# One decoder layer on one core, its program put in order by the scheduler's second timing model

## The chip, the cores and the metric

The kernel runs on one core of one Trainium2 chip. The metric is the device time of one execution in microseconds (us): 3150.36 us before the change, the median of three runs. In what follows PE is TensorE (the matmul engine), DVE is VectorE, ACT is ScalarE, POOL is GpSimd and SP is SyncE, which issues most of the transfers.

## The reference: what is computed

One layer for 2048 tokens of width 1024, all in float32. One projection feeds four mixers; their outputs pass through an output matrix and a layer norm; then come a mixture of 32 experts and a gated embedding, and a second layer norm.

```
u   = x @ W_in  (one combined projection; columns split among four parallel head groups)
y_A = RWKV-7 time mixing (4 heads x 64)       y_B = chunked gated linear attention (4 heads, dk 32, dv 64)
y_C = chunkwise mLSTM (4 heads x 64)          y_D = multi-head latent attention with decoupled rotary key (4 heads, dv 64)
x   = LN(alpha * x + concat(y_A, y_B, y_C, y_D) @ W_out)
x   = LN(alpha * x + HMoE(x) + sigmoid(x W_g + b_g) * (p[i] @ W_p))
HMoE: top-1 expert group, then top-2 SwiGLU experts inside that group.
```

## The kernel before

**Products.** A float32 product is made in three passes over rounded halves (`mm3`, L57 to L61: high by high at L59, and the two mixed ones at L60 and L61). The halves are made by `split`: a cast on ACT (L51) and a subtraction on DVE or POOL (L52).

**Order of the work.** The program is written with Tile: the code issues instructions in an order, and a scheduler then makes each engine's list. It is a list scheduler. It keeps a model of when each engine comes free and when each result is there; when an engine is free by that model, it takes, of the instructions that are ready by it, the one with the best priority, and an earlier place in the code is a better priority. So the code's order ranks the work, and the model's durations and delays decide how much lower-ranked work is put between two steps of a chain. On the chip every engine then works through its list in order and waits at each instruction for what that needs. Memory is taken from pools that are opened and closed in the code; tiles of a pool that is opened over the room of a closed one wait until the old tiles are done with.

**Mixers.** `layer()` steps through the projections in two halves of the tokens, in blocks of up to 256 columns (`proj`, L102), whose products go to the PSUM tile pbank. Between blocks it takes steps of the RWKV mixer from a generator (`rwkv`, L620), which uses the PSUM tiles abank and bbank. `rwkv_pre` (L380) prepares a piece of 256 tokens: sums of squares at L415, a chain of small DVE operations for their inverse roots (rk_iv, L68 to L73, called from there) and the decay factors, and products with the result at L423. `rwkv_b` (L526) solves a tile's triangular systems in dependent sub-steps (L541, L545, L550, L555, L562, L568). At block `LAST_AT` of the second half the rest of RWKV is written, its pools are closed, and the attention's normalized inputs and latents (`mla_norms` L1094 with the column sums at L1106, `mla_latents` L1118; PSUM tile sbank) are written between the last blocks:

```
            if n == L.LAST_AT:
                for _ in r:
                    pass
                rw.close()
                L.mla_pools(mla)
...
                L.mla_early(early)
                d = L.mla()
            if 0 <= n - L.LAST_AT < 4:
                next(d)
                L.gla_pre(n - L.LAST_AT)
        pr.close()
        L.gm_pools(gm)
        early.close()
        L.mla_more(mla)
```

After `pr.close()` the mLSTM mixer (`mlstm`, L924; PSUM tile cbank, state update L970 to L975) and the gated linear attention (`gla`, L733; PSUM tile gbank, first product L745, masked copy L747) get their pools in the room of the projections. `L.mla_more` opens the attention's pool in the room of the latents' pool, so no query of the attention starts before the last latents are made. Then 16 rounds of eight steps of attention (queries `mla_query` L1182 with scores at L1205, keys and values `mla_attend` L1225), one step of GLA and one of mLSTM follow.

**Output and experts.** `out_proj` (L1384, product at L1408) and `ple` (L1557) follow, and then `moe` (L1851). In a step of its loop, expert e's first block of 128 tokens goes through the gate and up weights (`moe_gu`, L1794, 48 products at L1801); a second block only if it exists, behind a branch at L1922; the down weights of expert e-1 follow (`moe_dn`, L1827, products at L1833, copies of the result on ACT at L1840). The hidden values m_t and the next tokens m_xg are turned by PE at L1350 and split again by L51 and L52. The weights are cast on ACT (L1771) and their low halves made on DVE or POOL (L1772). The branch at L1928 looks for third blocks on four engines. At last `finish` (L2117) and `norm2` (L2143) write the output.

Of the kernel before, what the change touches and what calls it, by code (L numbers as in the profile page):

```python
# [20 lines left out]
D = 1024  # L21
# [9 lines left out]
class Layer:  # L31
# [44 lines left out]
    # feature-major column tiles of w_in (start column, width)  # L76
# [4 lines left out]
    # columns that the token shift mixes, with their place in its weights  # L81
# [20 lines left out]
    def proj(self, h, blocks):  # L102
        """one half of the tokens against some of the columns, a block at a time"""
# [91 lines left out]
    # the columns that a causal convolution and silu follow  # L195
    CONV = "mq0", "mq1", "mk0", "mk1"

    def conv(self, i, p, y, more):
        """the taps carry a factor 1/2"""
# [73 lines left out]
    def sigmoid(self, out, in_, bias=0.0):  # L273
        """out = 0.5 + 0.5 tanh((in + bias2)/2), bias = bias2 / 2"""
        self.nc.scalar.activation(out, in_, AF.Tanh, bias=bias, scale=0.5)
        self.nc.gpsimd.tensor_scalar(out, out, 0.5, 0.5, op0=OP.mult, op1=OP.add)
# [34 lines left out]
    def rwkv_consts(self):  # L311
# [28 lines left out]
        # masks over [j, i]: same chunk of 64, strict / inclusive, block off the 32-diagonal  # L340
# [19 lines left out]
        # row mu of partition quarter s holds row m = 4 mu + s of the transposed inverse  # L360
# [7 lines left out]
        # products of a tile's tokens, zero between its two chunks  # L368
# [11 lines left out]
    def rwkv_pre(self, q):  # L380
        """scaled operands of the chunks and the inverses of the diagonal 32-blocks"""
# [112 lines left out]
    def rwkv_a(self, q, tt):  # L494
        """token-major operands and the masked products of a tile's chunks, four heads together"""
# [30 lines left out]
    def rwkv_b(self, q, tt):  # L526
        """solves, the chain over the chunks, the tile's outputs"""
# [92 lines left out]
    def rwkv(self):  # L620
        """the group in steps: operands run ahead of the products, and these ahead of the chain"""
# [45 lines left out]
    def log_sigmoid(self, z, out, t):  # L667
        """out = min(z, 0) - ln(1 + exp(-|z|)) for z in SBUF"""
# [22 lines left out]
    def gla_pre(self, q):  # L691
        """queries and keys times their chunk's decays, which go out to memory"""
# [86 lines left out]
    def gla_general(self):  # L779
        """Token by token, for decays too strong for the chunks' common scale."""  # L780
# [67 lines left out]
    def mlstm_gates(self):  # L848
        """gates of all chunks of 128, rows 16 h + c, and the running maxima"""
        nc = self.nc  # L850
        with ExitStack() as ctx:
# [39 lines left out]
            # own chunk's decay on the channels of each head  # L891
# [117 lines left out]
    def rope_tables(self):  # L1009
        """cos and sin (negated for the first half of a head's pairs) of position * frequency, for four heads' rows"""  # L1010
# [36 lines left out]
    def mla_consts(self):  # L1047
# [4 lines left out]
        # the heads' first 64 columns; their rotary columns; these with the pairs swapped  # L1052
# [10 lines left out]
        # the heads' key columns, then their value columns  # L1063
# [16 lines left out]
        # adds the two halves of the rows  # L1080
# [13 lines left out]
    def mla_norms(self, q):  # L1094
        """one over the latents' norms"""
# [22 lines left out]
    def mla_latents(self, q, cn, rs):  # L1118
        """latents over their norms; from them the values of all heads, and their queries and keys, which go out to memory"""
# [62 lines left out]
    def mla_query(self, hd, q):  # L1182
        """queries in two parts with the negated row maxima below them, in steps"""
# [11 lines left out]
        # any value near a row's maximum serves its softmax alike: the leading parts give it  # L1195
# [29 lines left out]
    def mla_attend(self, hd, q):  # L1225
        """even key tiles' products in the upper half of the rows, odd ones' in the lower half, at the same time"""
# [48 lines left out]
    def mla(self):  # L1275
        """the attention of a block of queries in steps, the next block's queries and keys made beside it"""
# [24 lines left out]
        for i, (hd, q) in enumerate(blocks):  # L1301
            while at <= i:
                at = next(ahead, 99)
            for _ in self.mla_attend(hd, q):
                work += self.LEAD
                # a head's keys lie over those of the head before the last
# [12 lines left out]
    ALPHA = 2.0 ** 0.25  # L1319

    def late_pools(self, ctx):
        """first norm's outputs in pairs of tiles, over them later an expert's gate and up weights; transposed blocks"""
        self.rc = self.pool(ctx, "rc")
        self.wgu = self.pool(ctx, "m_gu", 8)
        self.hl = self.pool(ctx, "hl", 2)
        self.psb = self.pool(ctx, "ps_b", 2, space=PSUM)
        self.mark = {}
# [4 lines left out]
    def weights(self, parts, n, scale=None, pool=None):  # L1332
        """128 rows of weights, put side by side, in leading and trailing parts"""
# [8 lines left out]
    def transpose_split(self, src, hi, lo, spread=False):  # L1342
        """[128, n] to [128, n/128, 128] in leading and trailing parts, rows 0 .. 63 and 64 .. 127 by turns in case of spread"""
# [113 lines left out]
    def pick(self, vals, mx, io, n, k, name):  # L1457
        """lowest index among the entries equal to the maximum, and its one-hot"""
# [11 lines left out]
    def route(self, t0, n, lg):  # L1470
        """tokens of tiles t0 .. t0 + n from logits [128, n, 36]"""
# [43 lines left out]
    def route_place(self, r):  # L1515
        """slots in the experts' lists, behind those of the earlier tiles"""
# [30 lines left out]
    # columns of router and gate side by side, in groups that fill a bank  # L1547
# [735 lines left out]
```

## Time and profile before

| what | value |
|---|---|
| median of three runs | 3150.36 us (3146.23 to 3152.82) |
| span of the profiled execution, first to last instruction | 3146.7 us |
| mean granted TensorE clock in it | 0.935 of full speed |
| PE busy | 2840.9 us, 90% of the span |
| DVE, ACT, POOL busy | 62%, 39%, 28% |
| DMA | 443.17 MB, mean 141 GB/s |

The profile gives the profiled execution's span and no other time of it; the median of the runs shown lies 3.7 us above that span. The span falls into the projections with RWKV (0 to about 909 us), the rest of the projections with the attention's latents (to 1064 and, with the first steps of mLSTM and GLA, 1103 us), the attention with mLSTM and GLA (to about 1585 us), the output projection and the gates (to about 2037 us), the experts (to about 3010 us), and the end. A busy share averages over these; so the prediction reads each stage by itself: PE's busy time, its granted clock, and what ended its waits.

### The profile page before, as it was taken

Reading aid. Unit: us, or ns where it says so; the run is one execution under the profiler, and the core shown is the slowest. Engines: PE = TensorE matmul, PEld = TensorE weight load, DVE = VectorE, ACT = ScalarE, POOL = GpSimd, SP = SyncE. Lnnn points to the kernel's source line nnn. Section 1 sums busy time; section 2 is a strip of 40 time slices with the busy share of each in tenths; the row PEclk is TensorE's granted clock in tenths of the full one; section 3 lists DMA queues with packets and bytes.
Section 4 is the critical chain, followed back from the end, with each engine's and each line's share of the span. In section 5 each row is a group of like instructions: output and inputs, shape, how many; then the busy total and the mean of one; then the engine's idle time right before and its main releaser. Section 6 shows DMA issues by size and latency. Waiting matters only on the chain. (4 is left out here: it accounts for less than half of the span.)

```text
span 3146.7 us, 42893 instructions
## 1 busy us (share of the span) xinstructions
PE 2840.9 (90%) x15420; PEld 2248.3 (71%) x15421; DVE 1955.0 (62%) x4094; ACT 1225.4 (39%) x2001; POOL 896.7 (28%) x552
## 2 busy tenths in 40 slices
PE   8999999998999899999999998789889988998883
PEld 6888888777877665566577797677667766776662
DVE  6366543566555466766656643467576767666869
ACT  4223232222134332323310121166575756666753
POOL 1000100111010033324421200346355545554525
PEclk9999999999998898989999998899999999999996
DMA  6332143122133612200243412188587867777873
GB/s 189 104 87 75 48 129 92 51 56 59 49 93 132 189 33 69 58 27 17 88 143 132 141 60 60 41 295 275 181 269 233 294 216 237 267 251 225 287 243 134
DMA packets 287054, 443.17 MB, mean 141 GB/s; under 512 B 84088, under 2 KB 152040, under 8 KB 286760
## 3 DMA queue, kind: packets, MB, share of 16 engines
q1 hardware_dynamic: 272200, 397.78, 38.3%
q0 software_dynamic: 14560, 41.47, 5.4%
q8 instruction: 184, 3.01, 0.4%
q14 instruction: 110, 0.90, 0.1%
HBM read 350.52 MB, written 96.50 MB: 142 GB/s over the span
## 5 line engine op out<-in xcount | busy, mean ns | idle before, releaser
L1801 PE MATMUL m_g<-m_g,xhl 128*128 128x512 f32 x2032 | 516.6, 402 | 14.7 <-PEq L1928 8.0
L1801 PEld LDWEIGHTS m_g<-m_g,xhl 128*128 128x128 f32 x2032 | 373.6, 191 | 105.9 <-issue 29.8
L1772 DVE TENSOR_TENSOR m_g<-m_raw,m_g 128x1024 fp32r<-128x1024 f32 x188 | 263.7, 1429 | 124.3 <-ACT m_g L1771 78.9
L1771 ACT CAST m_g<-m_raw 128x1024 fp32r<-128x1024 f32 x252 | 255.3, 1057 | 120.8 <-PEq L1928 105.3
L1833 PE MATMUL m_y<-m_dh,m_h 128*128 128x512 f32 x672 | 236.0, 415 | 24.6 <-PEq L1928 6.1
L59 PE MATMUL pbank<-xh,wh 128*128 128x512 f32 x544 | 220.7, 406 | 11.5 <-DVE us L209 8.2
L60 PE MATMUL pbank<-xl,wh 128*128 128x512 f32 x544 | 219.3, 403 | 0.0
L61 PE MATMUL pbank<-xh,wl 128*128 128x512 f32 x544 | 218.3, 402 | 0.0
L51 ACT CAST xhl<-bank 128x512 fp32r<-128x512 f32 x204 | 118.2, 607 | 251.6 <-PE bank L1350 244.0
L1772 POOL TENSOR_TENSOR m_g<-m_raw,m_g 128x1024 fp32r<-128x1024 f32 x64 | 182.8, 2940 | 89.6 <-ACT m_g L1771 50.5
L1408 PE MATMUL wide<-wt,xhl 128*128 128x512 f32 x768 | 183.4, 397 | 3.6 <-ACT xhl L51 3.6
L1772 POOL TENSOR_TENSOR m_dl<-m_raw,m_dh 128x1024 fp32r<-128x1024 f32 x64 | 177.9, 2814 | 22.1 <-ACT m_dh L1771 21.9
L1833 PEld LDWEIGHTS m_y<-m_dh,m_h 128*128 128x128 f32 x672 | 134.9, 201 | 58.7 <-issue 9.0
L1408 PEld LDWEIGHTS wide<-wt,xhl 128*128 128x128 f32 x768 | 143.7, 189 | 40.1 <-ACT xhl L51 7.4
L1248 POOL TENSOR_TENSOR mla_acc<-mla_acc,mla_pt 128x512 f32<-128x512 f32 (+3 forms) x112 | 135.7, 1212 | 117.4 <-ACT mla_pt L1246 101.1
L52 DVE TENSOR_TENSOR xhl<-bank,xhl 128x512 fp32r<-128x512 f32 x204 | 136.4, 685 | 49.3 <-ACT xhl L51 47.0
L1847 POOL DMA_INDIRECT accd<-m_y,m_put x47 | 94.6, 2013 | 249.6 <-ACT m_y L1840 135.5
L1588 PE MATMUL gate<-wt,xhl 128*128 128x354 f32 (+1 forms) x864 | 152.1, 333 | 14.3 <-DVE wide L1593 7.8
L1246 ACT ACTIVATE mla_pt<-sbank 128x512 f32<-128x512 f32 (+3 forms) x160 | 85.1, 533 | 202.7 <-PE sbank L1242 118.0
L1588 PEld LDWEIGHTS gate<-wt,xhl 128*128 128x128 f32 x864 | 144.1, 193 | 16.5 <-DVE wide L1593 8.6
L1833 PE MATMUL m_y<-m_dl,m_h 128*128 128x512 f32 x376 | 153.9, 409 | 0.0
L59 PE MATMUL pbank<-wh,xh 128*128 128x256 f32 x512 | 151.2, 295 | 0.0
(635 smaller groups left out, 6340.8 us busy)
## 6 DMA issues: line engine op xcount, KB each, us to landing
m_raw<-in_moe_w_down SPq DMA_DIRECT2D x64, 1024.0 KB
m_raw<-in_moe_w_gate SPq DMA_DIRECT2D x126, 512.0 KB
m_raw<-in_moe_w_up SPq DMA_DIRECT2D x126, 512.0 KB
wraw<-in_w_in SPq DMA_DIRECT2D x80, 256.0 KB
o_x<-in_x SPq DMA_DIRECT2D x16, 512.0 KB
x1d<-m_g SPq DMA_DIRECT2D x16, 512.0 KB
accd<-wide SPq DMA_DIRECT2D x16, 512.0 KB
m_raw<-accd SPq DMA_DIRECT2D x7, 1024.0 KB
```

What stands on the lines that cost most here:

```text
L51: nc.scalar.copy(hi, src)
L52: (eng and nc.gpsimd or nc.vector).tensor_sub(lo, src, hi.bitcast(F32))
L59: nc.tensor.matmul(out, lh, rh, start=start, stop=False)
L60: nc.tensor.matmul(out, lh, rl, start=False, stop=False)
L61: nc.tensor.matmul(out, ll, rh, start=False, stop=stop)
L1248: (nc.vector if kt in self.SUMS else nc.gpsimd).tensor_add(acc[:, c0 * 128:512], acc[:, c0 * 128:512], pt[:, 0:n])
L1408: nc.tensor.matmul(p[:, j], a[:, k], W[k][bb][:, j * 512:j * 512 + 512], start=k == 0 and i == 0, stop=k == 7 and i == 2)
L1588: nc.tensor.matmul(p[:, 0:n], a[:, k], b[:, o:o + n], start=k == 0 and i == 0, stop=k == 7 and i == 2)
L1771: self.nc.scalar.copy(h[:, i], raw[:, i])
L1772: lo_eng.tensor_sub(l[:, i], raw[:, i], h[:, i].bitcast(F32))
L1801: self.mark["pe"] = self.nc.tensor.matmul(banks[:, j], a, b[:, k % 2, j * 512:j * 512 + 512], start=k == 0 and i == 0, stop=k == 7 and i = ...
L1833: self.nc.tensor.matmul(p[:, j], a, b[:, k % 2, j * 512:j * 512 + 512], start=k == 0 and i == 0, stop=k == 3 and i == len(ps) - 1)
```

## The change

The context in which the whole program is built is told to use the scheduler's second timing model, which follows the instructions in a more detailed timeline:

```diff
-    with tile.TileContext(nc) as tc:
+    with tile.TileContext(nc, schedule_with_timeline_sim=True) as tc:
```

The rest of the difference drops comments and docstrings. No instruction is written differently and the priorities are the same; each engine's list comes out in another order. PE's list has 12520 lines of difference between the two orders, of some 10700 rows. Three places:

**PE in RWKV's solves.** Here PE's list stands in the second half of the tokens, in `rwkv_b`, from the last product of one sub-step (L550) over the next (L555) to the first of the one after (L562); pbank rows are the projections' products. Before:

```order
L550 MATMUL bbank<-xx,am_1029 128x128
L61 MATMUL pbank<-xh,wl 128x512
L59 MATMUL pbank<-xh,wh 128x512
L60 MATMUL pbank<-xl,wh 128x512
L61 MATMUL pbank<-xh,wl 128x512
L555 MATMUL bbank<-v_6281,dt_1022 128x128 x4
L59 MATMUL pbank<-xh,wh 128x512
L60 MATMUL pbank<-xl,wh 128x512
L61 MATMUL pbank<-xh,wl 128x512
L59 MATMUL pbank<-xh,wh 128x512
L60 MATMUL pbank<-xl,wh 128x512
L562 MATMUL bbank<-am_1028,xx 64x128
```

And now, with the first and the last of the rows that stand between; "..." stands for rows of the same three lines:

```order
L550 MATMUL bbank<-xx,am_1029 128x128
L60 MATMUL pbank<-wl,xh 128x256
L61 MATMUL pbank<-wh,xl 128x256
L59 MATMUL pbank<-wh,xh 128x256
...
L59 MATMUL pbank<-wh,xh 128x256
L555 MATMUL bbank<-v_6281,dt_1022 128x128 x4
L60 MATMUL pbank<-wl,xh 128x256
...
L60 MATMUL pbank<-wl,xh 128x256
L562 MATMUL bbank<-am_1028,xx 64x128
```

Before, four projection products stand in the first gap and five in the second; now there are 33 and 28. Over the 16 solves the mean goes from 3.4 to 18.8 in the first gap and from 5.8 to 23.4 in the second. Between L415 and L423, of which there are eight pairs, it was 24 to 60 and is 38 to 96. RWKV's last product moves from well ahead of the projections' end to that end.

**PE at the end of the projections.** The sbank rows of L1106 are the column sums of `mla_norms`, 48 in all; mla_x holds the attention's inputs, and cbank rows belong to mLSTM. Before, they stand among the projections:

```order
L60 MATMUL pbank<-xl,wh 128x512
L1106 MATMUL sbank<-ones_8179,mla_x 128x1 x4
L61 MATMUL pbank<-xh,wl 128x512
L59 MATMUL pbank<-xh,wh 128x512
L60 MATMUL pbank<-xl,wh 128x512
L1106 MATMUL sbank<-ones_8179,mla_x 128x1 x4
L61 MATMUL pbank<-xh,wl 128x512
L59 MATMUL pbank<-xh,wh 128x512
L60 MATMUL pbank<-xl,wh 128x512
L1106 MATMUL sbank<-ones_8179,mla_x 128x1 x4
```

And now; the first row here is the last projection product of all:

```order
L61 MATMUL pbank<-wh,xl 128x256
...
L950 MATMUL cbank<-ident,c_k 128x128
L950 MATMUL cbank<-ident,c_z 128x128
L1106 MATMUL sbank<-ones_8179,mla_x 128x1 x24
L956 MATMUL cbank<-c_v,c_am 128x65 x4
L959 MATMUL cbank<-ml_st_8075,c_a 128x130
L959 MATMUL cbank<-ml_st_8076,c_q 128x130
L1127 MATMUL sbank<-ident,mla_rs 128x128 x8
L970 MATMUL cbank<-c_v,ml_kw 128x130 x2
L933 LDWEIGHTS identb
```

No row of L1106 is ahead of the projections' last product any more, and the latents (L1147 to L1170) follow these. From that product to the first score of the attention (L1205) PE's list held 26 products into cbank and 22 into gbank before; now it holds 199 of all 304 into cbank, 49 of all 165 into gbank, and 140 into sbank.

**ACT in a step of the expert loop.** m_y is a block's result, m_dh the high half of an expert's down weights, m_h the turned hidden values and xhl the turned tokens. Before:

```order
L1840 COPY m_y<-m_y 128x512
L1771 CAST m_g<-m_raw 128x1024 x2
L51 CAST m_h<-bank 128x4x2x64
L1771 CAST m_dh<-m_raw 128x1024 x2
L1840 COPY m_y<-m_y 128x512
L51 CAST xhl<-bank 128x4x2x64 x2
L1771 CAST m_dh<-m_raw 128x1024
L1902 UNCONDITIONAL_BRANCH
L1771 CAST m_dh<-m_raw 128x1024
L1968 UNCONDITIONAL_BRANCH
```

And now, the same step:

```order
L1840 COPY m_y<-m_y 128x512
L1771 CAST m_dh<-m_raw 128x1024 x4
L1840 COPY m_y<-m_y 128x512
L51 CAST m_h<-bank 128x4x2x64
L51 CAST xhl<-bank 128x4x2x64
L1902 UNCONDITIONAL_BRANCH
L1817 ACTIVATE m_t<-m_g_18055 128x512
L51 CAST xhl<-bank 128x4x2x64
L1968 UNCONDITIONAL_BRANCH
```

Of the four casts into m_dh two stood between the two copies of m_y, behind m_h's split, and two behind xhl's. Now all four stand between the copies and ahead of both splits, and the second half of xhl's split stands behind m_t (L1817), which takes the next expert's first block from PE. On PE, 2 to 10 of the 48 products of L1801 of a first block stood behind the branch on the second block before; now all 48 are ahead of it.

## Rows read from the trace of the kernel before

**Rows 1.** The page: span and busy time of the engines.
```profile
span 3146.7 us, 42893 instructions
...
PE 2840.9 (90%) x15420; PEld 2248.3 (71%) x15421; DVE 1955.0 (62%) x4094; ACT 1225.4 (39%) x2001; POOL 896.7 (28%) x552
```

**Rows 2.** By stage: us; busy of PE, PEld, DVE, ACT, POOL; clock, DMA share, GB/s.
```profile
0.00:909.00 909.00, 855.62 (x5991) 721.43 (x5993) 503.62 (x1494) 246.17 (x509) 79.58 (x101) 0.96 0.30 84
909.00:1064.00 155.00, 147.45 (x731) 114.50 (x730) 85.53 (x221) 66.83 (x111) 5.71 (x9) 0.89 0.43 134
1064.00:1103.00 39.00, 30.72 (x133) 20.82 (x131) 17.06 (x51) 11.84 (x27) 0.18 (x2) 0.69 0.82 245
1103.00:1607.00 504.00, 479.45 (x2292) 302.29 (x2291) 325.81 (x746) 156.80 (x319) 188.40 (x152) 0.92 0.19 55
```

**Rows 3.** Waits of PE, 0 to 909 us: total us, times, longest.
```profile
PE abank L423 <- DVE rk_iv L73: 16.8, 5, 5.0
...
PE abank L423 <- DVE eend L457: 4.6, 1, 4.6
PE abank L423 <- DVE gi L484: 4.4, 1, 4.4
```

**Rows 4.** PE in order of time, 700 to 716 us: start, us, instruction, idle before.
```profile
715.65 0.69 PE L423 MATMUL abank<-ident,rk_iv 128*64 128x128 f32 x4 [4.65 <-DVE eend L457]
```

**Rows 5.** Busy time by stretch around that gap; columns as in rows 2.
```profile
659.00:697.00 38.00, 36.81 (x358) 29.63 (x356) 20.95 (x68) 6.33 (x19) 0.11 (x1) 1.00 0.16 39
697.00:713.00 16.00, 13.47 (x64) 10.18 (x63) 15.55 (x57) 6.65 (x14) 6.57 (x5) 1.00 0.18 59
713.00:724.00 11.00, 8.35 (x40) 7.27 (x40) 6.23 (x19) 1.10 (x2) 2.25 (x2) 0.53 0.22 60
```

**Rows 6.** PE, tile pbank by stage: length, busy (instructions), granted clock, DMA, GB/s.
```profile
0.00:909.00 909.00, 543.48 (x2775) 0.96 0.30 84
909.00:1064.00 155.00, 79.10 (x439) 0.89 0.43 134
1064.00:1103.00 39.00, 5.54 (x44) 0.69 0.82 245
```

**Rows 7.** The same for tile sbank.
```profile
909.00:1064.00 155.00, 75.50 (x279) 0.89 0.43 134
```

**Rows 8.** The same for tile cbank.
```profile
1064.00:1103.00 39.00, 9.06 (x48) 0.69 0.82 245
1103.00:1607.00 504.00, 89.79 (x512) 0.92 0.19 55
```

**Rows 9.** The same for tile gbank.
```profile
1064.00:1103.00 39.00, 16.77 (x39) 0.69 0.82 245
1103.00:1607.00 504.00, 55.06 (x204) 0.92 0.19 55
```

**Rows 10.** PE in order of time, 1069 to 1077 us.
```profile
1075.61 2.04 PE L745 MATMUL gbank<-gl_qz,g_k 128*128 128x512 f32 x2 [4.01 <-DVE gl_qz L743]
```

**Rows 11.** Busy time behind that gap; columns as in rows 2.
```profile
1076.00:1099.00 23.00, 19.01 (x55) 11.06 (x55) 7.64 (x22) 1.54 (x5) 0.00 (x0) 0.50 0.99 292
```

**Rows 12.** PE in order of time, 1583 to 1588 us.
```profile
1585.01 3.36 PE L1408 MATMUL wide<-wt,xhl 128*128 128x512 f32 x9
```

**Rows 13.** Groups of ACT, 2037 to 3010 us: count, busy us, mean ns.
```profile
L1771 ACT CAST m_dh<-m_raw 128x1024 fp32r<-128x1024 f32 x125 | 128.7, 1067 | 0.0
```

**Rows 14.** Waits of PE, 2037 to 3010 us.
```profile
PE bank L1350 <- PEq L1928: 19.3, 9, 7.2
PE bank L1350 <- DVE m_h L52: 12.3, 5, 4.3
PE bank L1350 <- DVE m_t L1819: 11.0, 7, 3.5
PE bank L1350 <- issue: 10.9, 4, 3.9
PE m_g L1801 <- PEq L1928: 8.0, 14, 1.4
```

## The prediction

> **What bounds the kernel now.** I read the busy times on the page first, then the table of stages, then the waits of the stages that the new order touches, then a few single gaps. TensorE (PE) is busy for 90% of the span and the next engine, DVE, for 62% [rows 1]. So the time is PE's work, plus what PE waits, plus what it loses at the lower clock. The table of stages [rows 2] lets me split each stage in that way. I call busy time times the granted clock "full-clock work". In 0 to 909 us (projections and RWKV) it is 855.62 x 0.96 = 821 us; the idle time is 909 - 856 = 53 us, and the other 35 us are loss at half clock. So full-clock work fills 90% of that stage, 131 of 155 us = 85% of the next, 441 of 504 us = 87% of the attention stage, and only 21 of 39 us = 54% between 1064 and 1103 us. That last stretch is what PE looks like when only the small matmuls of mLSTM and GLA are left to it.
>
> **Where it is lost.** In the first stage half of the idle time stands before one line, L423: 16.8 + 4.6 + 4.4 = 25.8 us in 7 waits [rows 3]. PE has multiplied at L415, and DVE's chain of small operations to L423 is still running when the projections that stand between run out; one such gap, of 4.65 us, stands in [rows 4]. The clock follows: 1.00 before that gap and in the stretch that ends in it, 0.53 in the 11 us with its end [rows 5]. Each such gap thus costs itself and about half of the 10 us after it.
>
> **The change, part by part.** One flag is set; no instruction's work changes. Each engine's list is put in another order, and nothing else. PE keeps its matmuls and SP its transfers, number for number; ACT loads a function table 21 times instead of 23, which I cost at nothing, since ACT is busy for 39% [rows 1] and hidden by PE. The loads of mLSTM and GLA wait on SP for the projections' memory in either order. Three places carry the sum.
>
> *Projections and RWKV (gain).* A projection matmul costs 543.48 / 2775 = 0.20 us of PE's time [rows 6]. Before, 24 to 60 of them stand between L415 and L423; now 38 to 96. Where it was 30 it is now 44 to 60, that is 14 to 30 more, or 2.8 to 6 us of cover against waits of 3.6 us on average. In the solves (L550 to L555 to L562) 3 to 6 became 19 to 23 on average. I take 28 of the 53 us of idle time away, 15 of them at L423, and leave 10 of the 35 us of clock loss. The price is that nothing is left over: before, RWKV is through within the first 909 us, and 79 + 6 us of projections are left after it [rows 6], under which the latents of the attention are computed; now RWKV and the projections end together. So all projection work belongs to this stage: 821 + 79.10 x 0.89 + 5.54 x 0.69 = 895 us [rows 6], + 25 idle + 10 clock = 930 us. At the old idle and clock loss it would be 983, with neither 895.
>
> *Between the projections and the attention (loss).* The attention's pool lies over the latents' pool, so no query can start before the last latents. Now those 48 column sums (L1106) and all latents come after the last projection. Until the first attention score (L1205) PE has no large matmuls at all: the sbank work, 75.50 x 0.89 = 67 us [rows 7]; 199 of the 304 cbank matmuls of mLSTM, (9.06 x 0.69 + 89.79 x 0.92) x 0.65 = 58 us [rows 8]; and 49 of the 165 gbank matmuls of GLA, (16.77 x 0.69 + 55.06 x 0.92) x 0.30 = 19 us [rows 9]. That is 144 us of full-clock work in small, dependent pieces. At the 85% that the latents reach with projections among them it takes 170 us; at the 54% of 1064 to 1103 us it takes 265 us. That stretch began with a 4.01 us wait for DVE [rows 10] and then ran 23 us at 0.50 clock [rows 11]. Now three chains (latents, mLSTM, GLA) fill PE where there were two, and latents' matmuls are 512 wide, so I stand between: a mean clock of 0.77, halfway from 0.69 to 0.85, gives 144 / 0.77 = 187 us, and with 28 us of waiting, 13% where the old stretch had 21%, it is 215 us. This is the least certain term.
>
> What the Trainium skill says of this, in "TensorE: Matmul & The Clock Gate" (section "Why this matters for your kernels"), speaks against the change: an array that pauses between bursts of matmuls drops to half rate, so bursts should be kept together. The pair [rows 10, 11] agrees. By that rule alone the estimate for this stretch would be the half clock throughout, 2 x 144 = 288 us.
>
> *Attention.* Full-clock work from 1103 us to the first output projection at 1585 us [rows 12] is 441 - 22 x 0.87 = 422 us; with 21 - 4 = 17 us from the stretch before, less the 77 us of mLSTM and GLA that moved ahead, 362 us remain. At 90%, as in the first stage, that is 402 us (at 87%, 416). I say 400, since fewer small pieces stand among the attention's. The output projection then starts at 930 + 215 + 400 = 1545 us instead of 1585: **-40 us**.
>
> *Output projection, gates, tail.* Their lists hold the same rows in nearly the same places; nothing but loads change neighbours (late loads of the tail on SP, a few accd loads ahead of p loads). I cost that at nothing, +-15 us; the first stage's cover is not needed there, since the weights of the output projection are loaded before.
>
> *The expert loop.* Two things get worse and one better. On ACT all four casts of the down weights (m_dh, 1067 ns each [rows 13]) now stand ahead of the splits of m_h and xhl, where before two stood between and two behind; and xhl's second half also comes after m_t, which waits for the next expert's whole first block. PE waits for these splits only where a second block is computed; by the count of down products between two first blocks in the trace, in 15 of the 31 steps. Most of the up to 4.3 us of casts runs beside products that PE has queued; what shows I put at a cast and a bit, 1.25 us x 15 = +19 us. Second, before, 2 to 10 of an expert's gate and up matmuls were left over to stand around the branch of L1928, and now all 48 are ahead of the branch on the second block. Waits on that branch are 19.3 + 8.0 = 27.3 us now [rows 14]; a third more is +9 us. Third, the turn of the second block's hidden values moves behind more matmuls, so that the waits for m_h and m_t (12.3 + 11.0 us [rows 14]) should halve: -12 us. Sum **+16 us**. From below: those two and the 10.9 us of "issue" vanish and nothing is added, -34 us. From above: two extra casts held in each of 31 steps, 31 x 2.1 = +65 us.
>
> **Sum.** The profiled execution's span is 3146.7 us [rows 1]; 3146.7 - 40 + 16 = 3123 us. The median of the runs is 3150.4, 3.7 us more than this span, so **3126 us**, 0.8% faster. A measurement of this kernel tells 0.2%, 6 us, from no change.
>
> **Rivals.**
> - *Half clock between projections and attention.* If each short wait there pulls the clock down again before the pieces can raise it, the stretch takes 265 us instead of 215: 3126 + 50 = 3176 us, slower. It decides from 239 us on: there the gain of 24 us is gone. For it: the 39 us that show such work alone [rows 2]. Against: those had no latents in them, and their one long wait was at the start. The page named above gives the same result, or a still later one. Chance 0.22.
> - *The casts on ACT hold every step of the expert loop*, also those without a second block, because the copies of the result free the bank behind them: +65 instead of +16 us, 3175 us, slower. For it: all four casts now need the down weights' transfer to have landed before the split. Against: PE has the 48 products of the next first block queued meanwhile. Chance 0.12.
> - *Both places go well*: 170 us between the stages and the waits of the loop only reduced (-12): 3126 - 45 - 28 = 3053 us. Chance 0.12.
> - *The filler is merely moved*: what the first stage gains is paid back in the second to within a few us, and the loop is unchanged: 3150 us. Chance 0.08.
>
> **How the numbers follow.** My forecast keeps 0.46, with its own range from 3080 (190 us between the stages, loop at 0) to 3165 (240 us, loop at +30). About 0.8 of it lies below 3144, a tenth within 0.2%, a tenth above. Faster: 0.46 x 0.8 + 0.12 = 0.49. Same: 0.05 + 0.08 = 0.13. Slower: 0.05 + 0.22 + 0.12 = 0.38 or so. The range that leaves out 2 in 10 goes from the good case, 3053, to a little above the two slow ones, 3190.
>
> **What would show it.** Right: in the first 930 us PE is idle for about 25 us, with L423 nearly gone from the waits and clock 0.98; then a stretch without pbank of about 215 us with clock near 0.77, before L1205; the output projection starts near 1545 us; the expert loop is 0 to 30 us longer, with splits of L51 held by m_dh casts. Wrong: pbank matmuls that end after 960 us (then DVE or ACT cannot keep RWKV's pace and the cover was not what PE lacked); a stretch before L1205 beyond 239 us; or a loop that changes by more than 40 us, which would say that my reading of the branch and the casts is at fault.

## The result, and the profile after

The changed kernel takes 3265.93 us (median of 4 runs, 3255.5 to 3274.08) against 3151.59 us before (median of the 4 runs beside it): a ratio of 1.0391, with a 95% interval from 1.0365 to 1.0416. It is 3.9% slower, where 0.8% faster was forecast, and lies above the range of 3053 to 3190 us. The page after, and its table of stages (us; busy of PE, PEld, DVE, ACT, POOL; clock, DMA share, GB/s), follow; the stages are cut at the projections' last product, the first attention score, the first output projection, the first expert product and PE's last product:

```profile
span 3262.6 us, 42873 instructions
...
PE 2918.2 (89%) x15419; PEld 2284.2 (70%) x15421; DVE 1880.1 (58%) x4094; ACT 1228.9 (38%) x1999; POOL 858.1 (26%) x552
```

```profile
0.00:945.00 945.00, 917.34 (x6472) 780.12 (x6473) 523.61 (x1513) 259.09 (x533) 60.79 (x87) 0.97 0.29 85
945.00:1173.00 228.00, 185.76 (x754) 134.66 (x752) 146.11 (x443) 78.76 (x155) 27.88 (x30) 0.70 0.47 143
1173.00:1630.00 457.00, 449.98 (x1828) 243.18 (x1826) 225.46 (x531) 140.46 (x270) 167.03 (x145) 0.91 0.13 39
1630.00:2078.00 448.00, 414.23 (x2164) 359.96 (x2164) 246.80 (x680) 74.23 (x118) 77.41 (x55) 0.96 0.31 101
2078.00:3214.00 1136.00, 950.86 (x4208) 766.28 (x4208) 693.88 (x848) 667.05 (x915) 499.67 (x226) 0.91 0.70 229
```

The same cuts before fall at 1070, 1103, 1585, 2051 and 3106 us; the last three stages then read:

```profile
1103.00:1585.00 482.00, 457.68 (x2199) 284.75 (x2197) 316.78 (x725) 155.13 (x316) 187.13 (x151) 0.92 0.17 50
1585.00:2051.00 466.00, 421.95 (x2174) 367.26 (x2174) 250.15 (x679) 72.96 (x118) 79.86 (x55) 0.94 0.29 96
2051.00:3106.00 1055.00, 927.38 (x4200) 739.57 (x4200) 745.47 (x858) 665.52 (x918) 525.26 (x228) 0.95 0.75 248
```

So the order ends the projections and RWKV at 945 us, starts the attention's scores at 1173 us where it was 1103 us, and is 45 us behind at the output projection [rows 12], 27 us behind at the first expert product, and 108 us behind at PE's last product; the end behind that takes 49 us instead of 41. In the expert loop two waits of PE stand out, at the branch on L1928 and for the split of m_h (total us, times, longest; before they are [rows 14]):

```profile
PE m_y L1833 <- PEq L1928: 68.1, 22, 6.5
PE bank L1350 <- DVE m_h L52: 39.5, 31, 4.1
PE bank L1350 <- PEq L1928: 10.7, 2, 5.5
```

The attention shows no wait of size. There a line of the costliest groups tells it: the value products (count of records, two to an instruction; busy us, mean ns), in the attention's stretch before and after.

```profile
L1222 PE MATMUL obank<-mla_pt,mla_v 128*64 128x512 f32 (+3 forms) x320 | 108.5, 565 | 0.0
```

```profile
L1222 PE MATMUL obank<-mla_pt,mla_v 128*64 128x512 f32 (+3 forms) x320 | 153.1, 577 | 0.0
```

One such product is no longer than before (577 against 565 ns). All together they hold PE for 153.1 us instead of 108.5. That is overlap lost: `mla_pv` writes the product of an even key tile to rows 0 to 63 of a bank and that of an odd one to rows 64 to 127, and two neighbours in PE's list run at the same time. In the list before, 55 of the 160 instructions follow their like directly; in the new list 9 do. (That each product is now taken as soon as its own exponentials are ready is a likely reason; no run tests it.) In the new trace 143 instructions stand alone and hold PE for 1.02 us each; in the trace before, the 44 pairs hold it for 1.02 us a pair. So 46 partners lost make 47 us, and the two rows differ by 44.6. (The 142 us and the 0.89 us in the expectations below leave out what lies under other products.)

### The profile page after: what moved, and what is told of

Read it like the earlier page. It is cut to its first block, busy times and chain, and to the rows that moved or that the text cites. A ratio compares the mean times of both kernels' runs of the same rounds, so it can differ in the third digit from the quotient of the medians.

```text
span 3262.6 us, 42873 instructions
## 1 busy us (share of the span) xinstructions
PE 2918.2 (89%) x15419; PEld 2284.2 (70%) x15421; DVE 1880.1 (58%) x4094; ACT 1228.9 (38%) x1999; POOL 858.1 (26%) x552
## 5 line engine op out<-in xcount | busy, mean ns | idle before, releaser
L1801 PE MATMUL m_g<-m_g,xhl 128*128 128x512 f32 x2032 | 504.6, 400 | 16.1 <-DVE m_t L1819 9.4
L1801 PEld LDWEIGHTS m_g<-m_g,xhl 128*128 128x128 f32 x2032 | 382.1, 192 | 100.4 <-ACT m_g L1771 12.5
L1833 PE MATMUL m_y<-m_dh,m_h 128*128 128x512 f32 x672 | 243.4, 426 | 105.6 <-PEq L1928 68.1
L1772 DVE TENSOR_TENSOR m_g<-m_raw,m_g 128x1024 fp32r<-128x1024 f32 x188 | 227.4, 1236 | 155.8 <-ACT m_g L1771 147.7
L1833 PEld LDWEIGHTS m_y<-m_dh,m_h 128*128 128x128 f32 x672 | 140.3, 209 | 144.7 <-issue 89.1
L1772 POOL TENSOR_TENSOR m_g<-m_raw,m_g 128x1024 fp32r<-128x1024 f32 x64 | 171.8, 2969 | 25.4 <-DVE m_g L1772 12.6
L1248 POOL TENSOR_TENSOR mla_acc<-mla_acc,mla_pt 128x512 f32<-128x512 f32 (+3 forms) x112 | 127.0, 1134 | 139.3 <-ACT mla_pt L1246 134.4
L1833 PE MATMUL m_y<-m_dl,m_h 128*128 128x512 f32 x376 | 161.3, 429 | 0.0
L1209 DVE TENSOR_REDUCE mla_m<-mbank 128x1 f32<-128x512 f32 (+3 forms) x160 | 94.0, 606 | 109.5 <-PE mbank L1205 63.9
L1222 PE MATMUL obank<-mla_pt,mla_v 128*64 128x512 f32 (+3 forms) x320 | 153.1, 577 | 0.0
```

Of the source, the lines that this page charges most:

```text
L1222: self.nc.tensor.matmul(po[k % 2 * 64:k % 2 * 64 + 64, c * 128:512], self.v1[:, k, hd, :], x, start=k < 2, stop=k >= nk - 2, skip_group_ch ...
L1248: (nc.vector if kt in self.SUMS else nc.gpsimd).tensor_add(acc[:, c0 * 128:512], acc[:, c0 * 128:512], pt[:, 0:n])
L1772: lo_eng.tensor_sub(l[:, i], raw[:, i], h[:, i].bitcast(F32))
L1801: self.mark["pe"] = self.nc.tensor.matmul(banks[:, j], a, b[:, k % 2, j * 512:j * 512 + 512], start=k == 0 and i == 0, stop=k == 7 and i = ...
L1833: self.nc.tensor.matmul(p[:, j], a, b[:, k % 2, j * 512:j * 512 + 512], start=k == 0 and i == 0, stop=k == 3 and i == len(ps) - 1)
```

## The experiments

All ratios are to runs of the kernel before that were taken beside each run (medians of 3144.69 to 3148.28 us), with 95% intervals; gains in us are differences of medians. Where a stage's length is given without a row, it is the distance of the same cuts in that run's trace.

### One cause in the attention: the pairs

```diff
-        for k, c, x in (pair.pop(0), pair.pop(0)):
-            self.nc.tensor.matmul(...)
+        odd = None
+        for k, c, x in (pair.pop(1), pair.pop(0)):
+            m = self.nc.tensor.matmul(...)
+            if odd:
+                self.tc.add_manual_dep(m.ins, odd.ins.name, ..., reason="the pair together")
+            odd = m
```

The product that becomes ready last is written first and the other one is ordered behind it, so that both are ready at once.

> The changed kernel, with one thing put back: the two value products of a pair of key tiles (L1222), which write the two halves of a bank's rows, stand side by side in PE's list again (78 pairs and one run of four, where the changed order has 9 such neighbours and the order before has 55). Theory (the attention lost 57 us against my sum because parted halves no longer run at the same time, PE's time per L1222 record going from 0.316 to 0.445 us): the stretch from the first score to the output projection falls from 457 to about 415 us, L1222 takes some 85 to 100 us of PE instead of 142, and the whole goes from 3266 to about 3220 us. Rival (the stretch is long because of the clock and of what else stands in it): no change, 3260 to 3270 us.

Measured: 3213.86 us, ratio 1.0231 (1.0183 to 1.0279), 52 us less. The stretch from the first score to the output projection (table of stages) and the value products in it (their line has moved by one):

```profile
1163.00:1571.00 408.00, 395.34 (x1826) 241.10 (x1825) 232.29 (x534) 139.81 (x269) 170.22 (x145) 0.86 0.14 44
```

```profile
L1223 PE MATMUL obank<-mla_pt,mla_v 128*64 128x512 f32 (+3 forms) x320 | 89.1, 614 | 0.0
```

457 us became 408, and 153.1 us of PE became 89.1. The clock of the stretch even fell, from 0.91 to 0.86, and PE's other busy time there was 297 us and is 306, so neither half of the rival explains the gain. The same edit on the old order:

> The kernel before, with the pairs of L1222 put side by side in PE's list (71 pairs and 3 runs of four, against 55 neighbours). Theory: 25 more products run beside their partner at 0.89 us each, so about 20 us less, 3130 us (0.7% faster). Rival (in the old order the single ones were filled by other work that now waits): no change, 3150 us.

Measured: 3121.42 us, ratio 0.9931 (0.9905 to 0.9958), 27 us less where 20 were expected. The old order had itself given away 25 partners; its stretch went from 482 to 463 us.

```profile
L1223 PE MATMUL obank<-mla_pt,mla_v 128*64 128x512 f32 (+3 forms) x320 | 84.5, 568 | 0.0
```

### Inside the expert loop: the splits and the branch

What the loop looks like after the change, around one of the steps (DVE, then PE, in order of time; start, us, instruction, idle before):

```profile
2549.07 5.83 DVE L1772 TENSOR_TENSOR m_dl<-m_raw,m_dh 128x1024 fp32r<-128x1024 f32 x2
2554.93 0.75 DVE L1842 SCALAR_TENSOR_TENSOR m_y<-m_y,m_half 64x512 f32<-64x512 f32 x1
2555.71 0.69 DVE L52 TENSOR_TENSOR m_h<-bank,m_h 128x512 fp32r<-128x512 f32 x1
```

```profile
2552.00 1.17 PE L1801 MATMUL m_g<-m_g,xhl 128*128 128x512 f32 x4
2556.46 1.12 PE L1350 MATMUL bank<-ident,m_xg 128*128 128x128 f32 x4 [3.29 <-DVE m_h L52]
2562.57 0.76 PE L1833 MATMUL m_y<-m_dh,m_h 128*128 128x512 f32 x1 [4.99 <-PEq L1928]
```

DVE makes both m_dl halves ahead of m_h's subtraction, which frees the bank that PE needs for the next turn: PE stands for 3.29 us. (The two take 5.83 us here; the 64 of the loop take 1.64 us each on average.) Then PE passes the branches on L1968 and L1928 one right behind the other, and stands for 4.99 us; its own record of L1928 is 4.33 us long. The 14 waits there of over 4 us end 0.47 to 0.52 us behind PE's own record, so what PE waits for is its own branch. PE's records of L1928, before and after (shortest, median and longest ns; the DVE, ACT and POOL records of the same branch are 39 to 68 ns in both):

```profile
L1928 PEldq COMPARE_BRANCH  x33: 70/437/6948, 2059.9 to 3028.3; - x33
```

```profile
L1928 PEldq COMPARE_BRANCH  x33: 70/3611/5182, 2094.0 to 3143.4; - x33
```

Two edits aim at one of the waits each. The first puts the down weights' casts behind the last split in ACT's list (`cut_at` is that split's cast; the subtractions follow the casts):

```diff
-            DW[e] = [self.split_piece(self.d_tiles(), r, g) for r, g in zip(R, (nc.vector, nc.gpsimd))]
+            last, D_ = self.cut_at, [self.d_tiles() for _ in R]
+            for r, (h, l), g in zip(R, D_, (nc.vector, nc.gpsimd)):
+                for i in range(2):
+                    m = nc.scalar.copy(h[:, i], r[:, i])
+                    if e + 1 < experts:
+                        tc.add_manual_dep(m.ins, last.ins.name, ..., reason="behind the turns' splits")
+                    g.tensor_sub(l[:, i], r[:, i], h[:, i].bitcast(F32))
+            DW[e] = D_
```

> The changed kernel with the casts of the down weights on ACT put behind the splits of m_h and xhl (order on ACT only; the subtractions into m_dl on DVE follow them). Theory (the subtractions into m_dl and the casts into m_dh, ahead of the splits, hold the bank that the next turn needs, in every step): the wait of PE for m_h, 38.3 us in 30 times, falls below 8 us, and with the clock that follows such waits the whole falls by 30 to 50 us, to 3216 to 3236 us. Rival (the wait only moves: what is saved ahead of the branch of L1928 is waited behind it, since the down products then wait for their weights): 3260 to 3270 us, with a wait of L1833 for m_dh or m_dl in its place.

Measured: 3234.39 us, 1.0282 (1.0240 to 1.0324), 32 us less, at the upper end of the theory's 3216 to 3236. The wait for m_h went from 39.5 us to 5.2; the waits at the branch stayed, 76.6 us for 78.8, but most of them are now put down to ACT:

(The lines of the loop stand 8 lower in this kernel; L1936 is the branch.)

```profile
PE m_y L1833 <- ACTq L1936: 60.4, 13, 4.7
PE m_y L1833 <- PEq L1936: 16.2, 12, 5.9
...
PE bank L1350 <- DVE m_h L52: 5.2, 1, 5.2
```

One of these waits in order of time (ACT, then PE):

```profile
2478.26 3.88 ACT L1891 CAST m_dh<-m_raw 128x1024 fp32r<-128x1024 f32 x4
```

```profile
2482.32 0.55 PE L1833 MATMUL m_y<-m_dh,m_h 128*128 128x512 f32 x1 [4.65 <-ACTq L1936]
```

PE's own record of the branch ends at 2479.04 us here, ACT's four casts at 2482.14, and L1833 starts at 2482.32. In all 13 waits L1833 starts 0.18 us behind ACT's last cast, and 0.7 to 4.0 us behind PE's own record. So the down products now wait until ACT is through the casts of the down weights, as the rival had it, while the time fell as the theory had it.

The second edit leaves out the branch where no third block exists, also the one behind the last expert:

```diff
-            third(e - 1)
+            if e in THIRDS:          # (5, 6, 17, 18)
+                third(e - 1)
...
-        third(e)
```

> The changed kernel without the branch of L1928 in 28 of 32 places, where no third block exists for this input; the four places where it is taken stay, so the work done is the same. Theory (in the new order nothing is queued on PE between the branch on the second block and that of L1928, so PE stands still 4 to 6.5 us each time, and the clock falls behind it): the waits on L1928, 68.1 and 10.7 us, fall to under 15 us, the clock of the expert loop rises from 0.91 to 0.95 or more, and the whole falls by 70 to 110 us, to 3155 to 3195 us. Rival (PE would wait at the same place for ACT or DVE anyway): by under 30 us, 3236 us or more.

Measured: 3233.91 us, 1.0280 (1.0227 to 1.0333), 32 us less and not 70 to 110: nearer the rival. All waits at L1928 are gone and the loop's clock is 0.94 for 0.91, yet PE now waits for the next expert's weights, which ACT, DVE and POOL prepare:

```profile
PE m_g L1801 <- POOL m_g L1772: 40.0, 22, 2.8
...
PE m_g L1801 <- ACT m_g L1771: 16.2, 20, 1.0
```

So a good part of the 78.8 us at the branch had hidden another lateness. All three edits at once:

> The changed kernel with the three edits at once: pairs of L1222 side by side, casts of the down weights behind the splits, and the branch of L1928 only in the four places where it is taken. Theory (three separate losses): the gains add, 52 + 32 + 32 us, so about 3150 us, and the expert loop is some 60 us shorter than in the changed kernel. Rival (the casts and subtractions of the weights are the bound of the loop once PE no longer stands at the branch, as the 40.0 us of waits for POOL's m_g in the run without the branch suggest, and putting the down casts behind the splits does not help then): 3175 us or more.

Measured: 3255.34 us, 1.0370 (1.0332 to 1.0409). The attention kept its gain (397 us), but the loop became longer than in any of the three, 1180 us against 1105 to 1138 (1136 in the changed kernel). My theory of separate losses fell here, and the rival held. PE now waits for the weights' low halves:

```profile
PE m_y L1838 <- POOL m_dl L1901: 49.0, 28, 4.6
PE m_g L1806 <- DVE m_g L1777: 44.8, 30, 2.0
```

The costliest groups of DVE show one reason: the subtraction into m_g, after the change and here.

```profile
L1772 DVE TENSOR_TENSOR m_g<-m_raw,m_g 128x1024 fp32r<-128x1024 f32 x188 | 227.4, 1236 | 155.8 <-ACT m_g L1771 147.7 <-PE bank L1350 6.7 <-DVEq L1928 0.5
```

```profile
L1777 DVE TENSOR_TENSOR m_g<-m_raw,m_g 128x1024 fp32r<-128x1024 f32 x188 | 419.1, 2276 | 13.8 <-ACT m_g L1776 13.3
```

188 equal subtractions take 2276 ns each instead of 1236. In that trace 42 of the 260 weight subtractions on DVE lie under POOL's subtractions for over 80% of their time and take 3.51 us on average, and the 124 that lie clear of them 1.22 us. After the change it is 18 at 2.81 us and 216 at 1.22 us, and before it 44 at 2.03 us and 169 at 1.22 us. So DVE and POOL subtract at the same time less after the change than before it, and this is not what made the changed kernel's loop longer; it came with the three edits. An edit that mends one wait makes the scheduler shift the others, and edits of single places could not settle the loop.

The branch in the old order:

> The kernel before without the branch of L1928 in the 28 places where no third block exists. Theory (the branch's long form, over 1 us on PE in 11 of 33 places before and in 19 after, costs 37 us in the old order and 80 us in the new): 20 to 30 us less than before, 3120 to 3128 us, that is about as much less as the new order gained, or a little less. Rival (old order hides it behind queued products): under 8 us, 3140 us or more.

> The kernel before with the pairs of L1222 side by side and without the branch of L1928 where it is not taken. Theory (separate places): the two gains add, 3121 us less 20 to 30 us, so 3091 to 3101 us. Rival (the loop is bound by its weights once the branch is gone): 3110 to 3121 us.

Measured: 3129.94 us, 0.9968 (0.9950 to 0.9987), and with the pairs 3114.68 us, 0.9911 (0.9881 to 0.9940). Both gain less than the theory said: 15 us (0.3%) for the branch alone, between theory and rival, and beside the pairs no more than can be told, inside the rival's range. In the old order the branch costs little. There products were still running on PE when it came to L1928 in 18 of the 19 places that follow L1968, after the change in none.

### The order of the loop as a whole

The last group holds engines to neighbours from the other kernel's lists. A table of instruction numbers, written in the kernel, gives each engine's old sequence; from it come dependences that order and do not wait:

```diff
+    got = {i.name: i for i in tc.nc.cur_bb.bb.instructions}
...
+        for step in part.split(":")[1].split(","):
+            at += int(step)
+            i = got.get(f"I-{at}")
...
+            if prev is not None:
+                tc.add_manual_dep(i, prev.name, info, reason="the other order's neighbours")
+            prev = i
```

> The changed kernel, but from the expert loop on every engine's list is held to the neighbours that it had before the change (a table of instruction numbers, as order without waits); mixers, output projection and gates stay in the new order. Theory (the loop's order alone costs the 80 to 90 us that the loop grew by): 3266 less 80 to 90, 3175 to 3190 us, the loop back at about 1055 us to its last down product. Rival (the loop is slower because of what it inherits: a later start of its weight loads, or the clock): 3230 us or more.

Measured: 3170.25 us, 1.0091 (1.0063 to 1.0120), 96 us less than the changed kernel, 5 us below what the theory gave. The loop takes 1049 us to PE's last product, 6 us less than before the change, with waits like the old ones:

```profile
PE bank L1350 <- PEq L1928: 23.0, 9, 7.0
PE bank L1350 <- DVE m_h L52: 15.6, 7, 4.2
```

It starts 20 us later than in the kernel before, and what it inherits does not matter. Next, which engines' lists it is:

> As the run before, but only ACT, DVE and POOL are held to their old order in the expert loop; PE's and SP's lists come from the second model, and PE keeps the products of the first block ahead of the two branches as in the changed order. Theory (two separate parts: splits held behind the weights' casts and subtractions on ACT and DVE, and PE's uncovered branch; the run that put the casts behind the splits gained 32 us): about half of the loss goes, 3215 to 3240 us, and PE still waits 50 us or more at L1928. Rival A (the order of the vector engines is the whole cause, and PE's branch only shows where PE waits anyway): 3180 to 3195 us. Rival B (it is PE's): 3250 us or more.

> As two runs before, but only PE is held to its old order in the expert loop; ACT, DVE, POOL and SP follow from the second model. Theory (PE's branch is covered again by 2 to 10 products, the splits stay late): the wait on L1928 falls from 78.8 to under 40 us, 3215 to 3240 us. Rival A (the vector engines are the cause): 3250 us or more. Rival B (PE's order is the whole cause): 3180 to 3195 us.

Measured: 3223.74 us (1.0256, 1.0228 to 1.0283) with ACT, DVE and POOL in the old order, as the theory had it, with 53.1 us left at the branch; and 3314.14 us (1.0562, 1.0522 to 1.0602) with PE in the old order alone, which no theory had:

```profile
PE m_y L1833 <- PEq L1928: 53.1, 21, 6.7
```

```profile
PE bank L1350 <- DVE m_t L1819: 128.5, 47, 7.4
PE bank L1350 <- DVE m_h L52: 20.5, 13, 5.8
```

PE's old list asks for the turn of the hidden values early; with DVE's and ACT's new lists these are late, and PE waits 128.5 us for m_t. So the loss is not one engine's: the lists of ACT, DVE and POOL are worth 42 us, those of PE and SP the other 54 once theirs are in place, and PE's old list alone makes the kernel 48 us slower still. PE's part and SP's were not separated.

### What is left of the change, and better versions

> The kernel before with the pairs of L1222 side by side, and with the output projection and the gates held to the order that the second model gave them, in which that stage took 448 us instead of 466. Theory (that gain belongs to the order of that stage): 3121 less 10 to 18 us, 3103 to 3111 us, the best of all so far. Rival (it came from what the stage inherits from the attention): no gain, 3118 to 3125 us.

Measured: 3109.77 us, 0.9898 (0.9866 to 0.9930). The stage took 456 us, against 467 with the pairs alone and 466 to 469 in all four traces with the old order: the gain is that order's own. The whole, against 3121.42 us with the pairs alone, is not clear of noise: the intervals of the two overlap.

> The changed kernel with both repairs: pairs of L1222 side by side, and the expert loop in its old order on every engine. Theory (the loss of the change is these two, in separate stages, and the rest of it is a gain of some 30 us): 3170 less 52, 3112 to 3125 us, about 1% faster than before. Rival (the repairs overlap, as the three repairs inside the new order did): 3140 us or more.

Measured: 3113.99 us, 0.9886 (0.9854 to 0.9919), as the theory had it: the two repairs add. The two best versions cannot be told apart. Of the 31 us below the kernel before, most is not the new order's merit, though: the old order with the same pairs takes 3121.42 us. At equal pairs the mixers end later in the new order (first output projection at 1577 us against 1561 us), the output projection and the gates are 11 us shorter, and the loop, in the same order, took 1039 us against 1049.

## Why the prediction was wrong, point by point

- **Projections and RWKV: right in kind, 15 us too low.** 930 us forecast, 945 measured, with 28 us of idle time (25 forecast). The clock loss is the term that was too small: I left 10 us, and at 0.97 it is about 27 (917.34 x 0.03). The waits at L423 fell from 25.8 us [rows 3] to 5.0:

```profile
PE abank L423 <- DVE rk_iv L73: 5.0, 4, 1.5
```

- **Between the projections and the attention: right in kind, 13 us too low.** 228 us for 215. The work was less than I had (185.76 x 0.70 = 130 us of full-clock work, for 144), the clock lower (0.70 for 0.77) and the waiting longer (42 us for 28). The stretch gives 130 / 228 = 57%, close to the 54% of the 39 us that I had seen [rows 2]; the middle that I chose was too hopeful. It was also badly made: 0.85 was the fill of the latents' stage, idle time included, and not its clock (0.89), and I added waiting on top. Of the 42 us idle 27 fall in the first 40 us:

```profile
945.00:965.00 20.00, 2.47 (x9) 1.24 (x7) 6.28 (x37) 0.60 (x1) 9.31 (x15) 0.57 0.55 160
965.00:1005.00 40.00, 30.68 (x135) 28.27 (x136) 20.24 (x79) 11.42 (x25) 1.97 (x4) 0.50 0.65 175
1005.00:1025.00 20.00, 19.57 (x92) 12.16 (x90) 11.37 (x29) 8.00 (x19) 0.00 (x0) 0.98 0.43 147
1025.00:1045.00 20.00, 18.30 (x79) 15.88 (x78) 15.97 (x41) 9.85 (x16) 0.78 (x2) 0.53 0.55 165
```

Behind a first 20 us with hardly any work the granted clock was 0.50 (the level of 1.2 GHz) for 40 us, then 0.98 (close to 2.4 GHz) for 20 us, then 0.53. The Trainium skill's rule that pauses between bursts bring the half rate ("TensorE: Matmul & The Clock Gate", section "Why this matters for your kernels") agrees with the start of the stretch; half clock throughout, the 288 us that the prediction drew from it, did not come.
- **Attention: this step failed.** I had it as work over a fill of 90%, 400 us; it took 457. The fill was right (449.98 x 0.91 = 409 us in 457, 90%), the work was not: "full-clock work" took PE's busy time before as an amount that an order cannot change. Part of it rested on pairs that ran at the same time, and I did not look at where the value products stand in the new list, although it was there to be read. Of the 47 us of work above my 362, the parted pairs are 44.6 x 0.91 = 41. With the pairs put back the stage took 408 us, so the term's sum would have held, though by luck in part: less work than I had (395.34 x 0.86 = 340 us) at a lower fill (83%).
- **Output projection and gates: 18 us better** than the nothing that I had, just beyond its bounds of 15. The end behind PE's last product, in the same term, took 8 us more.
- **Expert loop: this step failed, too.** +16 us forecast, with bounds of -34 and +65; to PE's last product it grew by 81 us. The rival of the casts was half right: PE waits for the splits in 31 places (39.5 us), and I had counted 15 steps. What holds them is the casts on ACT and the subtractions on DVE behind these; no run separates the two. The branch was priced at a third more and became the largest wait of the loop, 68.1 + 10.7 = 78.8 us against 33.4 before (19.3 + 8.0 of [rows 14], and 6.1 in a row below them). That the products which covered it are gone was right in kind; what I mis-sized is the branch without them, whose records on PE are 84.7 us in all where they were 45.0. The clock went with the waits: 0.95 to 0.91. Which of these waits makes what part of the 81 us stays open: the loop's old order on all engines takes all of it back, and either repair alone about 30 us of it.
- **The chances.** The rival of half clock named the right stretch, at 265 us where it took 228; I had called this the least certain term. What made the kernel slower were two other terms, of which I held the attention's for known. And the mixers' gain of 40 us would not have come even with the attention as it was: the three stages before the output projection took 15, 13 and 57 us more than I had, and with the pairs put back still 8, 11 and 8 us more, while the old order with its pairs put back gains 24 us there, too.

## What to carry to other kernels

When a scheduler's order changes, busy time is no constant: look for instructions that run at the same time only as neighbours, and count the neighbours in the new list. Look for waits that two engines' lists settle together, like the split of a turn, and for branches that lose the work queued ahead of them. And hold one stage to the other order before mending single places in it: one run showed that the loop's order is its whole loss, where three plausible repairs each gained 32 to 52 us and together 11.

## What the runs showed of the hardware

- **Half-height products run at the same time only as neighbours.** Alone one holds PE for 1.02 us (143 places after the change) and two neighbours together for 1.02 us (44 pairs before it); with 78 pairs side by side all 160 hold it for 89.1 us, 0.56 us each. The Trainium skill describes products in separate groups of columns as concurrent ("TensorE: Matmul & The Clock Gate", section "Why this matters for your kernels"); the runs agree, and add that an instruction between the two costs the overlap.
- **The branch on L1928 is often long on PE where PE comes to it from the branch on L1968.** In the changed kernel's trace L1928 starts within 1 us of the end of L1968's record in 18 of 33 places, and in 16 of these its record is 3.25 to 5.18 us long. That one branch is near another does not explain it: in 13 other places L1928 starts within 0.17 us of the end of L1910's record, with products of L1801 still running, and only 3 of these take over 1 us. Nor must L1968 be that near: with ACT, DVE and POOL in their old order all 19 places behind it are 1.0 to 3.8 us away, and 14 still take 1.6 to 6.0 us. Before the change, with products still running at 18 of the 19, 10 take over 1 us. In the four places where PE goes on into the third block's code, the record is 70 to 78 ns in both kernels. The Trainium skill ("Runtime: NRT & Kernel Launch", section "Instruction fetch mechanics") says that a taken branch out of the fetched window waits for a transfer of instructions. That would fit, but no run here separates it from other causes.
- **DVE's subtraction of two SBUF tiles slows beside POOL's**, from 1.22 us to means of 2.03 us (before the change), 2.81 us (after it) and 3.51 us (all three edits) where it lies under one for over 80% of its time. The Trainium skill ("GPSIMD Engine Reference", section "1. Specifications") says that POOL shares its SBUF interfaces with such instructions of DVE; the traces agree.
